# The expert weights of a two-block layer, laid out in memory in the order in which the kernel loads them

## The chip, the cores and the metric

The kernel runs on one core of one Trainium2 chip. The metric is device time in microseconds (us) of one execution; lower is better. All data are fp32. A "chunk" below is one transfer of 1 MB (1,048,576 bytes) of weights from memory into a tile of 128 partitions with 8 KB each.

## The reference, cut to what matters

Two transformer blocks are applied to 256 tokens of width 1024. The second block ends in a mixture of 32 experts; each token goes to two of them. What the change touches is only this part:

```python
N_EXPERTS, EXPERT_TOPK, EXPERT_FF, D_MODEL = 32, 2, 512, 1024

def hier_moe(h, w_group, b_group, w_expert, b_expert, w1, w3, w2):
    # w1, w3: (32, 1024, 512); w2: (32, 512, 1024)
    ...
    def expert_block(args):
        xb, e = args
        hid = jax.nn.silu(xb @ w1[e]) * (xb @ w3[e])
        return hid @ w2[e]
    ...
```

The three expert tensors hold 3 x 32 x 1024 x 512 numbers, 192 chunks of 1 MB. Every execution reads all of them once.

## The kernel before

The program first computes block one, then the attention part of block two, then the router, and then walks over the experts in 8 groups of 4 (`for g in range(8)`, L1102). Tokens sit in 32 slots for each expert, so 4 experts fill the 128 columns of TensorE: `slot_mm` (L1090) issues 4 matmuls, one for each expert of the group, each on its own 32 columns, all with the same k-slice of the weights.

One group needs 24 chunks, in this order: 8 of w1 and 8 of w3 (one for each slice of 128 input features, each with 4 experts x 512 columns), then 4 of w2 for the first 512 output columns and 4 for the last 512. The last group (g = 7) takes its last 512 columns in two passes of 256 (`FINE`, L1098), so that its last 4 MB come as 8 transfers of 512 KB.

All expert weights come through `eload` (L1031). It takes the next tile of a rotation over 19 tiles of 8 KB per partition (`rings`, L825) and issues one transfer from the SP queue (L1034). The first group also finds two extra places for its last two w3 chunks; one of them is filled by two half transfers (`whalf`). SP issues in program order and waits, before a transfer, until the last reader of the tile is through. The order of instructions is chosen by a scheduler at build time. Some expert transfers are issued early, between loads of other weights (`wload`, L148); the others follow after SP has loaded the number `cnt` (L1047), which decides at g = 4 whether the branch for overfull experts (`overflow`, L1046) is taken. It was not taken in this execution.

The transfer itself is this:

```python
t = t[:, :ne * n].rearrange("p (e n) -> p e n", e=ne)
nc.sync.dma_start(out=t, in_=wd[g * 4 + e0:g * 4 + e0 + ne, k * P:(k + 1) * P,
                                c0:c0 + n].rearrange("e p n -> p e n"))
```

With n = 512 each partition receives four rows of 2 KB, one from each expert; in memory these rows lie 2 MB apart. With n = 256 (the last 8 transfers) the rows have 1 KB.

After the last expert chunk, PE finishes the last 256 columns, the last norm follows (L1163 to L1173), and two transfers write the result (L1174).

Of the kernel before, what the change touches and what calls it, by code (L numbers as in the profile page):

```python
# [18 lines left out]
P = 128  # L19
# [62 lines left out]
def block_kernel(ctx: ExitStack, tc: tile.TileContext, A, out: bass.AP):  # L82
# [22 lines left out]
    def t_tile(n):  # L105
        return psum.tile([P, 512], F32, name=n, tag="t", bufs=2)
# [28 lines left out]

    # weight chunks rotate over the slots that are open
    slots_of = {"list": [(ring, 4)], "i": 0}
# [19 lines left out]

    # operand pieces: rotate over the pools that are open
    base = (None, 3)
# [3 lines left out]
    def piece(v, a, b, after=(), eng=None):  # L163
        order = [p for p, n in homes["list"] for _ in range(n)]
        bufs = dict(homes["list"])
        pair = order[homes["i"] % len(order)]
        homes["i"] += 1
        if pair is None:
            # two pieces in a row share a slot for their low parts
            hi = dn.tile([P, a, b], F32R, name="whi", tag="whi", bufs=3)  # L170
            if low["n"] % 2 == 0:
                low["t"] = lows.tile([P, 2, 1024], F32R, name="wlo", tag="w")
            lo = low["t"][:, low["n"] % 2, :a * b].rearrange("p (a b) -> p a b", a=a)
            low["n"] += 1
        else:
            hi = pair.tile([P, a, b], F32R, name="whi", tag="whi", bufs=bufs[pair])
            lo = pair.tile([P, a, b], F32R, name="wlo", tag="wlo", bufs=bufs[pair])
        with ExitStack() as q:
            for ins in after:
                q.enter_context(tc.issue_after(ins.ins))  # L180
            split_to(hi, lo, v, eng)
        return hi, lo
# [8 lines left out]

    # features out on partitions: weights stationary, all tokens stream
    def t_block(dst, pc, c0, k, act):
# [10 lines left out]

    # tokens out on partitions: tokens stationary, weights stream
    def ts_pieces(src, c0, n, after=(), free=0, aside=()):
# [116 lines left out]

    # ------------------------------------------------------------------ first block: mixing
    w_in = A["w_in"][0]
# [25 lines left out]

    # pool mixer
    po = (mg1.tile([P, 4, S], F32R, name="poh"), mg1.tile([P, 4, S], F32R, name="pol"))
# [33 lines left out]

    # memory keys and values
    w = wload(rows(w_in, 0, KT, 2048, 256), KT, 256)
# [14 lines left out]

    # stick-breaking attention, keys on partitions
    sb = (mg1.tile([P, 4, S], F32R, name="sbh", tag="sbh"), mg1.tile([P, 4, S], F32R, name="sbl", tag="sbl"))
# [33 lines left out]

    # cross attention
    xo = (mg1.tile([P, 2, S], F32R, name="xoh"), mg1.tile([P, 2, S], F32R, name="xol"))
# [36 lines left out]

    # gated branches  # L480
    tg = {}
# [56 lines left out]

    # ------------------------------------------------------------------ feed-forward
    s1 = ExitStack()  # L540
# [20 lines left out]

    # first columns token-major, so that the first half of the tokens can run ahead
    h0 = (fp.tile([P, 4, S], F32R, name="h0h", bufs=1), fp.tile([P, 4, S], F32R, name="h0l", bufs=1))
# [46 lines left out]

    # ------------------------------------------------------------------ second block: mixing
    s2 = ExitStack()
# [47 lines left out]

    # index scores
    qiT = rope_heads(3072, 1.0, "qiT", at, 4, first[0], 2, (1,3))
# [126 lines left out]

    # router weights, with the gain of the norm before them  # L790
    wr = perm.tile([P, KT, 40], F32, name="wr")
# [41 lines left out]

    # ------------------------------------------------------------------ second block: experts
    nt = xp.tile([P, NT, D], F32, name="nt", tag="xhi")
# [161 lines left out]

    # gates
    nneg = ptile([P, NT, 2], "nneg")
# [27 lines left out]

    w1d, w3d, w2d = A["w1_2"][0], A["w3_2"][0], A["w2_2"][0]
    slots_of.update(list=rings, i=0)

    def eload(wd, g, k, c0, n):  # L1031
        def fill(t, e0, ne):
            t = t[:, :ne * n].rearrange("p (e n) -> p e n", e=ne)
            nc.sync.dma_start(out=t, in_=wd[g * 4 + e0:g * 4 + e0 + ne, k * P:(k + 1) * P,  # L1034
                                            c0:c0 + n].rearrange("e p n -> p e n"))
            return [t[:, e, :] for e in range(ne)]

        # places that only the first group's weights find free
        if g == 0 and wd is w3d and k == KT - 1:
            return fill(xp.tile([P, 2048], F32, name="wchunk", tag="xlo"), 0, 4)  # L1040
        if g == 0 and wd is w3d and k == KT - 2:
            return [r for e0 in (0, 2) for r in fill(dn.tile([P, 1024], F32, name="whalf", tag="whi", bufs=3), e0, 2)]
        return fill(chunk_tile(), 0, 4)

    # experts with more than CAP tokens: the tokens past the slots, over all experts
    def overflow():  # L1046
        cv = nc.values_load(cnt[0:1, 0:1], min_val=0, max_val=S)  # L1047
        with tc.If(cv > CAP):
# [11 lines left out]
            ow = dn.tile([P, D], F32, name="ovw", tag="whi", bufs=3)  # L1060
            with tc.For_i(0, NE, 1) as ei:
                for f in range(4):
                    bs = []
                    for wd in (w1d, w3d):
                        wt = ow.rearrange("p (k n) -> p k n", k=KT)
                        nc.gpsimd.dma_start(out=wt, in_=wd[bass.ds(ei, 1), :, f * P:(f + 1) * P].rearrange(
                            "o (k p) n -> p (o k) n", p=P))
                        b = t_tile("ovb")
                        for kt in range(KT):
                            nc.tensor.matmul(b[:, :S], lhsT=wt[:, kt, :], rhs=xT[:, kt, :], start=(kt == 0),  # L1070
                                             stop=(kt == KT - 1))
                        bs.append(b)
                    s = dn.tile([P, 512], F32, name="ms", tag="sqscr", bufs=1)
                    nc.scalar.activation(s[:, :S], bs[0][:, :S], AF.Silu)
                    nc.vector.tensor_tensor(out=hh[:, f, :], in0=bs[1][:, :S], in1=s[:, :S], op=ALU.mult)
                for hf in range(2):
                    o = acc_tile("ovo")
                    for f in range(4):
                        wt = ow[:, (f % 2) * 512:(f % 2 + 1) * 512]
                        nc.gpsimd.dma_start(out=wt, in_=w2d[bass.ds(ei, 1), f * P:(f + 1) * P,  # L1080
                                                          hf * 512:(hf + 1) * 512].rearrange("o p n -> p (o n)"))
                        for tt in range(NT):
                            nc.tensor.matmul(o[tt], lhsT=hh[:, f, tt * P:(tt + 1) * P], rhs=wt, start=(f == 0),
                                             stop=(f == 3))
                    for tt in range(NT):
                        xa = x[:, tt, hf * 512:(hf + 1) * 512]
                        nc.vector.scalar_tensor_tensor(out=xa, in0=o[tt], scalar=gov[:, tt, bass.ds(ei, 1)],
                                                       in1=xa, op0=ALU.mult, op1=ALU.add)

    def slot_mm(o, lhsT, w, first, last):  # L1090
        for e in range(4):
            ps = slice(e * 32, e * 32 + 32)
            nc.tensor.matmul(o[ps, :], lhsT=lhsT[:, ps], rhs=w[e], start=first, stop=last,  # L1093
                             skip_group_check=True, tile_position=(0, e * 32))

    # the last columns come in small parts, so that little is left to do behind the last weights
    WHOLE = ((0, 512), (512, 512))
# [4 lines left out]
    for g in range(8):  # L1102
# [4 lines left out]
        hb = acc_tile("hb")  # L1107
        for i, wd in enumerate((w1d, w3d)):
            for kt in range(KT):
                slot_mm(hb[i], xs[:, kt, :], eload(wd, g, kt, 0, EFF), kt == 0, kt == KT - 1)  # L1110
        s = dn.tile([P, 512], F32, name="ms", tag="sqscr", bufs=1)
# [22 lines left out]
        if g == 7:  # L1134
            # the gain of the last norm, on all partitions
            glx = xp.tile([P, 2, D], F32, name="glx", tag="xhi")
# [9 lines left out]
        for i, (c0, n) in enumerate(FINE if g == 7 else WHOLE):  # L1146
            cs = slice(c0, c0 + n)
            yb = t_tile("yb")
            for ft in range(4):
                slot_mm(yb[:, :n], hT[:, ft, :], eload(w2d, g, ft, c0, n), ft == 0, ft == 3)  # L1150
            nc.scalar.activation(y[:, cs], yb[:, :n], AF.Copy)  # L1151
# [11 lines left out]
    for tt in range(NT):  # L1163
# [15 lines left out]
        "w_in_2", "w_proj_a_2", "w_proj_b_2", "w_out_2", "g_ffn_2", "w_group_2", "b_group_2", "w_expert_2",  # L1179
        "b_expert_2", "w1_2", "w3_2", "w2_2", "g_final_2"]  # L1180
_OUTS = [((1, 256, 1024), "float32")]


# [17 lines left out]
```

## Time and profile before

| what | value |
|---|---|
| median of 3 runs | 1135.88 us (1135.5 to 1139.17) |
| span of the profiled execution | 1139.4 us |
| PE busy | 969.1 us (85%) |
| DVE busy | 447.6 us (39%) |
| ACT busy | 354.5 us (31%) |
| read from memory | 308.70 MB, 272 GB/s over the span |
| time of the packets on the SP transfers' queue | 77.0% of 16 DMA engines |

The profiled execution's span lies at the upper end of the three timed runs, 3.5 us above their median. PE's busy time is the sum of intervals in which some matmul was in its pipeline; it says little about a stage in which matmuls wait for each other's data. The page's second part cuts the span into 40 slices of 28.5 us and shows for each the busy share of the engines, the granted TensorE clock (PEclk, tenths of 2.4 GHz), the busy share of the 16 DMA engines and the rate of their transfers. The experts fill the last 17 of these slices.

### The profile page before, as it was taken

The numbers are of one execution on the slowest core, as the hardware profiler recorded it, in microseconds if no ns is written. First come the engines' busy times: TensorE is split into PE (matmuls) and PEld (weight loads), VectorE is DVE, ScalarE is ACT, GpSimd is POOL, SyncE is SP. The second block draws the span as 40 slices with busy tenths as digits, with TensorE's granted clock in tenths as the row PEclk, the third lists the DMA queues.
The fourth block names the chain that finished last, engine by engine and source line by source line (L and its number), as shares of the span: only waits on it lengthen the run. The fifth ranks groups of instructions, "written<-read, shape, count | busy, mean of one in ns | idle before, by whom it ended". The sixth has DMA issues, their size and how long they took to land. (4 is left out here: it accounts for less than half of the span.)

```text
span 1139.4 us, 14755 instructions
## 1 busy us (share of the span) xinstructions
PE 969.1 (85%) x6119; PEld 662.9 (58%) x6119; DVE 447.6 (39%) x750; ACT 354.5 (31%) x552; POOL 53.3 (5%) x45
## 2 busy tenths in 40 slices
PE   6999999999999998999999996875676676676665
PEld 5889989978999986788889842121121222112111
DVE  5555536676455446698547511100101010001102
ACT  4445655365444434445654410000000000000002
POOL 1000012120000003120000000000000000000000
PEclk9999999999999999999999999766778778767767
DMA  9844337767555326545457999999999999999996
GB/s 318 264 150 148 112 130 248 241 232 243 191 190 187 121 90 222 170 162 186 150 192 268 370 319 386 386 387 385 387 386 384 386 385 387 385 387 386 387 387 215
DMA packets 181349, 310.74 MB, mean 273 GB/s; under 512 B 11040, under 2 KB 62240, under 8 KB 181280
## 3 DMA queue, kind: packets, MB, share of 16 engines
q1 hardware_dynamic: 181280, 309.77, 77.0%
q8 instruction: 49, 0.80, 0.3%
q14 instruction: 20, 0.16, 0.0%
HBM read 308.70 MB, written 1.05 MB: 272 GB/s over the span
## 5 line engine op out<-in xcount | busy, mean ns | idle before, releaser
L156 DVE TENSOR_TENSOR wlo<-wchunk,whi 128x1024 fp32r<-128x1024 f32 (+1 forms) x180 | 222.9, 1240 | 160.0 <-ACT whi L155 157.5
L155 ACT ACTIVATE whi<-wchunk 128x1024 fp32r<-128x1024 f32 (+1 forms) x193 | 200.7, 1048 | 226.6 <-PE gu L186 55.8
L1093 PE MATMUL hb<-wchunk,xs 128*32 128x512 f32 x1016 | 168.5, 765 | 95.2 <-DMA wchunk<-in_w_dram 91.6
L1093 PEld LDWEIGHTS hb<-wchunk,xs 128*32 128x32 f32 x1016 | 26.3, 121 | 216.5 <-DMA wchunk<-in_w_dram 175.9
L1093 PE MATMUL yb<-wchunk,mw 128*32 128x512 f32 (+1 forms) x544 | 75.5, 672 | 31.3 <-DMA wchunk<-in_w_dram 29.1
L185 PE MATMUL gate<-xhi,whi 128*128 128x256 f32 x320 | 92.0, 287 | 0.6 <-DVE tg L508 0.6
L186 PE MATMUL gate<-xlo,whi 128*128 128x256 f32 x320 | 91.4, 286 | 0.0
L187 PE MATMUL gate<-xhi,wlo 128*128 128x256 f32 x320 | 91.3, 285 | 0.0
L187 PE MATMUL gu<-xhi,wlo 128*128 128x256 f32 x288 | 81.3, 282 | 0.0
L186 PE MATMUL gu<-xlo,whi 128*128 128x256 f32 x288 | 81.2, 282 | 0.0
L185 PE MATMUL gu<-xhi,whi 128*128 128x256 f32 x288 | 81.1, 282 | 0.0
L1156 DVE TENSOR_TENSOR x<-x,comb 128x512 f32<-128x512 f32 (+1 forms) x34 | 22.3, 656 | 140.5 <-PE comb L1154 140.5
L1093 PEld LDWEIGHTS yb<-wchunk,mw 128*32 128x32 f32 x544 | 14.8, 122 | 86.5 <-DMA wchunk<-in_w_dram 57.3
L185 PEld LDWEIGHTS gate<-xhi,whi 128*128 128x128 f32 x320 | 61.1, 191 | 3.4 <-issue 2.4
L1120 ACT ACTIVATE mw<-hT 128x512 f32<-128x512 f32 x8 | 4.8, 597 | 184.6 <-PE hT L1118 184.6
L987 DVE TENSOR_TENSOR xs<-gat,gk 128x512 f32<-128x512 f32 x16 | 11.1, 692 | 130.0 <-PE gat L979 130.0
L186 PEld LDWEIGHTS gate<-xlo,whi 128*128 128x128 f32 x320 | 61.1, 191 | 1.4 <-issue 1.3
L187 PEld LDWEIGHTS gate<-xhi,wlo 128*128 128x128 f32 x320 | 61.0, 191 | 1.4 <-issue 1.4
L185 PEld LDWEIGHTS gu<-xhi,whi 128*128 128x128 f32 x288 | 55.1, 191 | 0.3
L186 PEld LDWEIGHTS gu<-xlo,whi 128*128 128x128 f32 x288 | 54.8, 190 | 0.3
L187 PEld LDWEIGHTS gu<-xhi,wlo 128*128 128x128 f32 x288 | 54.8, 190 | 0.0
L1115 DVE TENSOR_TENSOR mw<-hb,ms 128x512 f32<-128x512 f32 x8 | 5.5, 692 | 115.8 <-PE hb L1093 115.8
(395 smaller groups left out, 1710.5 us busy)
## 6 DMA issues: line engine op xcount, KB each, us to landing
wchunk<-in_w_dram SPq DMA_DIRECT2D x187, 1024.0 KB, 14.4
wchunk<-in_w_in_dram SPq DMA_DIRECT2D x43, 1024.0 KB, 5.1
wchunk<-in_w_ffn_in_dram SPq DMA_DIRECT2D x22, 1024.0 KB, 5.2
wchunk<-in_w_ffn_out_dram SPq DMA_DIRECT2D x11, 1024.0 KB, 5.0
wchunk<-in_w_out_dram SPq DMA_DIRECT2D x8, 1024.0 KB, 5.9
wchunk<-in_w_dram SPq DMA_DIRECT2D x8, 512.0 KB, 9.2
wchunk<-in_w_mem_kv_dram SPq DMA_DIRECT2D x2, 1024.0 KB, 5.5
wchunk<-in_w_pool_o_dram SPq DMA_DIRECT2D x2, 1024.0 KB, 5.3
```

What stands on the lines that cost most here:

```text
L155: a = nc.scalar.activation(hi, src, AF.Copy)
L156: return a, (eng or nc.vector).tensor_tensor(out=lo, in0=src, in1=hi.bitcast(F32), op=ALU.subtract)
L185: nc.tensor.matmul(o, lhsT=lh[0], rhs=rh[0], start=start, stop=False)
L186: nc.tensor.matmul(o, lhsT=lh[0], rhs=rh[1], start=False, stop=False)
L187: return nc.tensor.matmul(o, lhsT=lh[1], rhs=rh[0], start=False, stop=stop)
L987: nc.vector.tensor_tensor(out=xss[g][:, ks, :], in0=b.rearrange("p (k t) -> p k t", k=4), in1=gk[:, ks, None].to_broadcast([P, 4, P]), op= ...
L1093: nc.tensor.matmul(o[ps, :], lhsT=lhsT[:, ps], rhs=w[e], start=first, stop=last, skip_group_check=True, tile_position=(0, e * 32))
L1115: nc.vector.tensor_tensor(out=h, in0=hb[1], in1=s, op=ALU.mult)
L1120: nc.scalar.activation(mw[:, 1, :], b, AF.Copy)
L1156: nc.vector.tensor_tensor(out=xa, in0=xa, in1=cb[:, :n], op=ALU.add)
```

## The change

A new function `expert_runs` rearranges the three expert tensors on the host, before the kernel starts, into one tensor `experts` of 192 pieces, each 128 x 2048 numbers, in the order (group, chunk). The device time does not contain it. For 20 of the 24 chunks of a group each partition's 8 KB lie in one run. For the 4 chunks of the last 512 output columns the piece is split into two halves of 256 columns, and each partition receives two runs of 4 KB; the last group loads these halves one at a time, as 512 KB with one run of 4 KB for each partition. Bytes, number of transfers, destination tiles and their rotation stay as they were. The two half transfers of the first group (`whalf`) now read runs of 4 KB.

In `slot_mm` the weights of an expert are now a view with one more dimension: (128, 1, 512), or (128, 2, 256) with the two pieces 4 KB apart in the tile. The `overflow` branch, not taken here, is rewritten to read the new tensor; its loop has 8 rounds with the work of 4 experts each instead of 32 rounds.

```diff
-    w1d, w3d, w2d = A["w1_2"][0], A["w3_2"][0], A["w2_2"][0]
+    ew = A["experts"].rearrange("(g c) p n -> g c p n", g=8)
+    W1, W3, W2 = 0, KT, 2 * KT
...
-    def eload(wd, g, k, c0, n):
+    def eload(g, c, part=None):
+        src = ew[g, c]
+        if c >= W2 + 4:
+
+            src = src.rearrange("p n -> (p n)").rearrange("(h p n) -> p h n", h=2, p=P)
+            if part is not None:
+                src = src[:, part:part + 1, :]
+
         def fill(t, e0, ne):
-            t = t[:, :ne * n].rearrange("p (e n) -> p e n", e=ne)
-            nc.sync.dma_start(out=t, in_=wd[g * 4 + e0:g * 4 + e0 + ne, k * P:(k + 1) * P,
-                                            c0:c0 + n].rearrange("e p n -> p e n"))
-            return [t[:, e, :] for e in range(ne)]
...
+            if c >= W2 + 4:
+                m = 2 if part is None else 1
+                v = t[:, :m * 1024].rearrange("p (h n) -> p h n", h=m)
+                nc.sync.dma_start(out=v, in_=src)
+                v = v.rearrange("p h (e n) -> p h e n", e=4)
+                return [v[:, :, e, :] for e in range(4)]
+            v = t[:, :ne * 512]
+            nc.sync.dma_start(out=v, in_=src[:, e0 * 512:(e0 + ne) * 512])
+            return [v[:, e * 512:(e + 1) * 512].rearrange("p (h n) -> p h n", h=1) for e in range(ne)]
...
     def slot_mm(o, lhsT, w, first, last):
         for e in range(4):
             ps = slice(e * 32, e * 32 + 32)
-            nc.tensor.matmul(o[ps, :], lhsT=lhsT[:, ps], rhs=w[e], start=first, stop=last,
-                             skip_group_check=True, tile_position=(0, e * 32))
...
+            m = w[e].shape[1]
+            nc.tensor.matmul(o[ps, :].rearrange("p (h n) -> p h n", h=m), lhsT=lhsT[:, ps], rhs=w[e], start=first,
+                             stop=last, skip_group_check=True, tile_position=(0, e * 32))
...
-                slot_mm(hb[i], xs[:, kt, :], eload(wd, g, kt, 0, EFF), kt == 0, kt == KT - 1)
+                slot_mm(hb[i], xs[:, kt, :], eload(g, c0 + kt), kt == 0, kt == KT - 1)
...
+def expert_runs(w1, w3, w2):
+
+    a = [w.reshape(8, 4, KT, P, EFF).transpose(0, 2, 3, 1, 4).reshape(8, KT, P, 2048) for w in (w1, w3)]
+    v = w2.reshape(8, 4, 4, P, 2, 512).transpose(0, 4, 2, 3, 1, 5)
+    lo = v[:, 0].reshape(8, 4, P, 2048)
+    hi = v[:, 1].reshape(8, 4, P, 4, 2, 256).transpose(0, 1, 4, 2, 3, 5).reshape(8, 4, P, 2048)
+    return np.concatenate([*a, lo, hi], axis=1).reshape(8 * 24, P, 2048)
```

No engine's instructions change place: the transfers stand where they stood between the other loads. This piece of SP's order, from the attention part of block two, shows it (rows with - are those of before, with + those after; a row names line, destination, source and the shape of one transfer).

```order
 L148 DMA wchunk<-in_w_in_dram 128x4x512 x2
-L1034 DMA wchunk<-in_w_2_dram 128x4x512 x2
+L1049 DMA wchunk<-in_experts_dram 128x2048 x2
 L148 DMA wchunk<-in_w_in_dram 128x4x512 x9
 L148 DMA wchunk<-in_w_in_dram 128x8x256 x4
-L1034 DMA wchunk<-in_w_2_dram 128x4x512
+L1049 DMA wchunk<-in_experts_dram 128x2048
 L148 DMA wchunk<-in_w_in_dram 128x8x256 x4
```

The shape is what moved: 128 partitions with four pieces of 512 numbers became 128 partitions with one piece of 2048. In both orders SP issues, after it has loaded `cnt`, 94 whole chunks ahead of the branch at g = 4, 72 behind it, and then the 8 transfers of 512 KB; 22 MB have been issued ahead of `cnt`.

## Rows read from the trace of the kernel before

**Rows 1.** The page's slices: granted clock and DMA share in tenths, rate, 28.5 us each.
```profile
PEclk9999999999999999999999999766778778767767
DMA  9844337767555326545457999999999999999996
GB/s 318 264 150 148 112 130 248 241 232 243 191 190 187 121 90 222 170 162 186 150 192 268 370 319 386 386 387 385 387 386 384 386 385 387 385 387 386 387 387 215
```

**Rows 2.** Waits from 655 us on: total us, times, longest us.
```profile
PEld hb L1093 <- DMA wchunk<-in_w_dram: 175.9, 71, 11.5
...
PE hb L1093 <- DMA wchunk<-in_w_dram: 91.6, 65, 10.6
PEld yb L1093 <- DMA wchunk<-in_w_dram: 57.3, 36, 2.9
```

**Rows 3.** Windows of the expert part: length, busy times, granted clock, DMA share, GB/s.
```profile
core 0: us, PE busy (x) PEld busy (x) DVE busy (x) ACT busy (x) POOL busy (x), PEclk, DMA share, GB/s
...
660.00:662.00 2.00, 2.00 (x24) 0.56 (x20) 0.00 (x0) 0.00 (x0) 0.00 (x0) 1.00 0.97 298
662.00:664.00 2.00, 2.00 (x24) 0.65 (x20) 0.00 (x0) 0.00 (x0) 0.00 (x0) 1.00 1.08 238
664.00:666.00 2.00, 2.00 (x24) 0.60 (x20) 0.00 (x0) 1.49 (x2) 0.00 (x0) 1.00 0.86 292
666.00:668.00 2.00, 2.00 (x24) 0.57 (x20) 0.00 (x0) 0.39 (x1) 0.00 (x0) 1.00 1.05 363
700.00:1100.00 400.00, 269.41 (x1430) 74.62 (x1428) 37.80 (x70) 14.33 (x24) 0.00 (x0) 0.74 1.05 386
...
1122.00:1124.00 2.00, 0.86 (x14) 0.16 (x8) 1.11 (x2) 1.00 (x3) 0.00 (x0) 1.00 1.08 365
```

**Rows 4.** DMA packets and bytes, 700 to 1100 us; issues with us to landing.
```profile
DMA packets 77639, 154.41 MB, mean 386 GB/s; under 512 B 2351, under 2 KB 2351, under 8 KB 77622
...
q1 hardware_dynamic: 77622, 154.16, 104.6%
...
wchunk<-in_w_dram SPq DMA_DIRECT2D x147, 1024.0 KB, 14.4
```

**Rows 5.** SP's wait for `cnt` and the transfers behind it, timeline.
```profile
658.44 42.17 SPq L1034 DMA_DIRECT2D wchunk<-in_w_dram  x18
```

**Rows 6.** Other weights: DMA slices, packets and issues, 366 to 385 us.
```profile
GB/s 0 0 69 69 190 414 414 448 423 181 0 0 17 0 78 95 103 414 414 414 423 267 0 0 0 0 129 78 354 414 431 414 371 52 0 0 0 29 152 233
DMA packets 961, 3.37 MB, mean 177 GB/s; under 512 B 63, under 2 KB 191, under 8 KB 959
...
wchunk<-in_w_ffn_out_dram SPq DMA_DIRECT2D x3, 1024.0 KB, 4.9
```

**Rows 7.** Windows ahead of the experts: two expert chunks, then w_ffn_out and w_out.
```profile
240.00:243.50 3.50, 3.50 (x17) 2.85 (x16) 3.50 (x3) 3.50 (x4) 2.91 (x2) 1.00 1.05 399
246.00:250.00 4.00, 3.91 (x17) 2.85 (x17) 3.33 (x6) 1.44 (x2) 0.56 (x1) 1.00 1.03 422
605.00:607.00 2.00, 2.00 (x19) 2.00 (x18) 1.32 (x2) 0.39 (x1) 0.00 (x0) 1.00 1.02 418
608.00:610.00 2.00, 2.00 (x19) 2.00 (x18) 2.00 (x4) 1.09 (x2) 0.00 (x0) 1.00 1.02 414
```

**Rows 8.** Expert matmuls in the timeline, first at 2.4 GHz, then at 1.2 GHz.
```profile
678.21 7.05 PE L1093 MATMUL yb<-wchunk,mw 128*32 128x512 f32 x64
...
714.93 1.93 PE L1093 MATMUL hb<-wchunk,xs 128*32 128x512 f32 x8 [0.79 <-DMA wchunk<-in_w_dram]
```

**Rows 9.** The chain that ended last, one group's pieces: start, us, what.
```profile
889.94 1.93 PE hb L1093 x8
891.87 2.75 PE gat L979 x13
...
910.87 0.70 DVE mw L1115
911.62 1.13 PE hT L1118 x4
912.77 0.61 ACT mw L1120
```

**Rows 10.** Groups of instructions from 655 us on: count, busy us, mean ns.
```profile
L1154 PE MATMUL comb<-ysb,mw 128*128 128x512 f32 x60 | 38.6, 773 | 8.1 <-ACT ysb L1151 8.1
```

**Rows 11.** The chain's end, from the last expert transfer on.
```profile
1120.20 8.43 DMA wchunk<-in_w_dram
1128.67 0.68 PE yb L1093 x8
...
1134.16 0.93 ACT fo L1173
```

**Rows 12.** Who held up the SP queue from 655 us on: us, times, longest us.
```profile
SPq L1034 <- PE hb L1093: 131.1, 75, 4.6
...
SPq L1034 <- PE comb L1154: 32.5, 14, 4.7
...
SPq L1047 <- DVE cnt L1026: 4.5, 1, 4.5
```

More of the change, by code (lines that the diff above doesn't have):

```diff
@@ L1026, in block_kernel @@
     nc.vector.tensor_copy(cnt, cmx)
-    w1d, w3d, w2d = A["w1_2"][0], A["w3_2"][0], A["w2_2"][0]
+    ew = A["experts"].rearrange("(g c) p n -> g c p n", g=8)
+    W1, W3, W2 = 0, KT, 2 * KT
     slots_of.update(list=rings, i=0)
-    def eload(wd, g, k, c0, n):
-        def fill(t, e0, ne):
-            t = t[:, :ne * n].rearrange("p (e n) -> p e n", e=ne)
-            nc.sync.dma_start(out=t, in_=wd[g * 4 + e0:g * 4 + e0 + ne, k * P:(k + 1) * P,
-                                            c0:c0 + n].rearrange("e p n -> p e n"))
-            return [t[:, e, :] for e in range(ne)]
-        if g == 0 and wd is w3d and k == KT - 1:
+    def eload(g, c, part=None):
[4 more added lines that the diff above has]
+                src = src[:, part:part + 1, :]
+        def fill(t, e0, ne):
+            if c >= W2 + 4:
[7 more added lines that the diff above has]
+            return [v[:, e * 512:(e + 1) * 512].rearrange("p (h n) -> p h n", h=1) for e in range(ne)]
+        if g == 0 and c == W3 + KT - 1:
             return fill(xp.tile([P, 2048], F32, name="wchunk", tag="xlo"), 0, 4)
-        if g == 0 and wd is w3d and k == KT - 2:
+        if g == 0 and c == W3 + KT - 2:
             return [r for e0 in (0, 2) for r in fill(dn.tile([P, 1024], F32, name="whalf", tag="whi", bufs=3), e0, 2)]
@@ L1060, in overflow @@
             ow = dn.tile([P, D], F32, name="ovw", tag="whi", bufs=3)
[L1061 to L1077, printed above, removed]
-                    for f in range(4):
-                        wt = ow[:, (f % 2) * 512:(f % 2 + 1) * 512]
-                        nc.gpsimd.dma_start(out=wt, in_=w2d[bass.ds(ei, 1), f * P:(f + 1) * P,
-                                                          hf * 512:(hf + 1) * 512].rearrange("o p n -> p (o n)"))
-                        for tt in range(NT):
[L1083 to L1088, printed above, removed]
@@ new lines, in overflow @@
+            gv = gov.rearrange("p t (g e) -> p t g e", g=8)
+            with tc.For_i(0, 8, 1) as gi:
+                for e in range(4):
+                    for f in range(4):
+                        bs = []
+                        for c0 in (W1, W3):
+                            wt = ow.rearrange("p (k n) -> p k n", k=KT)
+                            cs = slice(e * 512 + f * P, e * 512 + (f + 1) * P)
+                            nc.gpsimd.dma_start(out=wt, in_=ew[bass.ds(gi, 1), c0:c0 + KT, :, cs].rearrange(
+                                "o k p n -> p (o k) n"))
+                            b = t_tile("ovb")
+                            for kt in range(KT):
+                                nc.tensor.matmul(b[:, :S], lhsT=wt[:, kt, :], rhs=xT[:, kt, :], start=(kt == 0),
+                                                 stop=(kt == KT - 1))
+                            bs.append(b)
+                        s = dn.tile([P, 512], F32, name="ms", tag="sqscr", bufs=1)
+                        nc.scalar.activation(s[:, :S], bs[0][:, :S], AF.Silu)
+                        nc.vector.tensor_tensor(out=hh[:, f, :], in0=bs[1][:, :S], in1=s[:, :S], op=ALU.mult)
+                    for hf in range(2):
+                        o = acc_tile("ovo")
+                        for f in range(4):
+                            wt = ow[:, (f % 2) * 512:(f % 2 + 1) * 512]
+                            src = ew[bass.ds(gi, 1), W2 + hf * 4 + f]
+                            if hf == 0:
+                                src = src[:, :, e * 512:(e + 1) * 512].rearrange("o p n -> p (o n)")
+                                nc.gpsimd.dma_start(out=wt, in_=src)
+                            else:
+                                src = src.rearrange("o p n -> o (p n)").rearrange("o (h p n) -> p (o h) n", h=2, p=P)
+                                nc.gpsimd.dma_start(out=wt.rearrange("p (h n) -> p h n", h=2),
+                                                    in_=src[:, :, e * 256:(e + 1) * 256])
+                            for tt in range(NT):
+                                nc.tensor.matmul(o[tt], lhsT=hh[:, f, tt * P:(tt + 1) * P], rhs=wt, start=(f == 0),
+                                                 stop=(f == 3))
+                        for tt in range(NT):
+                            xa = x[:, tt, hf * 512:(hf + 1) * 512]
+                            nc.vector.scalar_tensor_tensor(out=xa, in0=o[tt], scalar=gv[:, tt, bass.ds(gi, 1), e],
+                                                           in1=xa, op0=ALU.mult, op1=ALU.add)
@@ L1107, in block_kernel @@
         hb = acc_tile("hb")
-        for i, wd in enumerate((w1d, w3d)):
+        for i, c0 in enumerate((W1, W3)):
             for kt in range(KT):
-                slot_mm(hb[i], xs[:, kt, :], eload(wd, g, kt, 0, EFF), kt == 0, kt == KT - 1)
+                slot_mm(hb[i], xs[:, kt, :], eload(g, c0 + kt), kt == 0, kt == KT - 1)
         s = dn.tile([P, 512], F32, name="ms", tag="sqscr", bufs=1)
@@ L1149, in block_kernel @@
             for ft in range(4):
-                slot_mm(yb[:, :n], hT[:, ft, :], eload(w2d, g, ft, c0, n), ft == 0, ft == 3)
+                w = eload(g, W2 + (4 if c0 else 0) + ft, c0 // 256 - 2 if n == 256 else None)
+                slot_mm(yb[:, :n], hT[:, ft, :], w, ft == 0, ft == 3)
             nc.scalar.activation(y[:, cs], yb[:, :n], AF.Copy)
@@ L1179 @@
         "w_in_2", "w_proj_a_2", "w_proj_b_2", "w_out_2", "g_ffn_2", "w_group_2", "b_group_2", "w_expert_2",
-        "b_expert_2", "w1_2", "w3_2", "w2_2", "g_final_2"]
+        "b_expert_2", "g_final_2"]
 _OUTS = [((1, 256, 1024), "float32")]
+def expert_runs(w1, w3, w2):
[4 more added lines that the diff above has]
+    return np.concatenate([*a, lo, hi], axis=1).reshape(8 * 24, P, 2048)
 def kernel(**inputs):
@@ L1190 @@
     named = [(n, np.ascontiguousarray(inputs[n])) for n in _INS]
+    named.append(("experts", expert_runs(*(np.asarray(inputs[n]) for n in ("w1_2", "w3_2", "w2_2")))))
     named += [(f"c{i}", a) for i, a in enumerate(_CONSTS)]
```

## The prediction

> **What bounds the kernel now.** I began with the page's slices [rows 1]. The last 17 of the 40 slices are the experts: there the transfer rate stands at 384 to 387 GB/s, slice after slice, with the DMA engines' share at 9 and over, while the granted clock of TensorE lies at 6 to 8 tenths. Nowhere earlier does the rate hold such a level. A flat rate under a changing clock says that the stage runs at the pace of the transfers. The waits from 655 us on say the same from the other side [rows 2]: PE's matmuls and weight loads of the experts wait for landing chunks, 71 times for w1 and w3 alone, up to 11.5 us at a time. The windows [rows 3] give the size: 386 GB/s over the 400 us from 700 to 1100, DMA share 1.05 (over 1 because an engine's packets overlap a little), clock 0.74. In this window 154.41 MB arrived [rows 4]; 77,622 - 2,351 = 75,271 packets of 2 KB and over make 154.15 MB, so they are the 2 KB rows. One chunk of 1.0486 MB takes 400 x 1.0486 / 154.41 = **2.716 us**, a group of 24 takes 65.2 us.
>
> The stage does not begin with the first expert chunk. 22 MB come early, beside a PE that is still busy with attention and the router; then SP waits for `cnt`, and only from 658.44 us on do the other 170 MB follow [rows 5]. What makes transfers faster before that moment is given back in the wait for `cnt`, which hangs on the router, not on DMA. So the change is worth what it does to 166 whole chunks and 8 halves.
>
> **What the row length is worth.** The trace has no 8 KB row in this queue. It has 4 KB rows: w_ffn_out and w_out come as two rows of 4 KB for each partition. Between 366 and 385 us three such chunks come alone (961 packets in all, 768 of them of 4 KB), and their slices of 0.475 us read 414, 414, 448, 423 and again 414, 414, 414, 423 [rows 6]. Longer windows in such transfers read 422, 418 and 414 [rows 7]. Two expert chunks of 2 KB rows, loaded just ahead of the first of these, read 399 in 3.5 us [rows 7], and over hundreds of us 386 [rows 3]: a short stretch shows some 3% more than a long one. The 1 KB rows of the end read 365 [rows 3]. So the rate rises with the row, 365, 386 to 399, 414 to 422: each row seems to cost something beside its bytes.
>
> Per engine (a sixteenth of the rate), a 2 KB row takes 2048 x 16 / 386 = 84.9 ns in the long run. A 4 KB row at 418 takes 156.8 ns; lowered by the 3% of long stretches (405 GB/s) it takes 161.8. The second 2 KB thus cost 71.9 to 76.9 ns instead of 84.9. If the third and fourth cost as much, 8 KB take 300.6 to 315.6 ns, which is 436 to 415 GB/s. Bounds: at least what long stretches of 4 KB rows should give (405: no further gain), at most 436. I take **420 GB/s** for 8 KB, near the value from long stretches because the whole stage is one, and **410** for 4 KB.
>
> A rule stands against the change. The Trainium skill, page "DMA: Bandwidth & Descriptors", section "Specifications", calls 512 bytes the least transfer for line rate; by it 2 KB rows are there already and the sum is 0. The trace disagrees: 2 KB rows hold 386 where 4 KB rows reach 414 to 422 [rows 3, 7]. The same page, section "Why small descriptors are slow", charges a fixed 3 cycles per packet on 32-byte beats; with its ceiling of 435 GB/s (an estimate) 2 KB would reach 416 and 8 KB 430, a gain of 3.3%, some 15 us here. The measured step from 2 KB to 4 KB alone is larger.
>
> **The sum.** A group has 20 chunks at 420 (2.497 us) and 4 at 410 (2.558 us), 2.507 us in the mean, 0.209 less than 2.716.
> - 166 whole chunks x 0.209 = 34.7 us.
> - From 660 to 668 us the rate is below 386 (298, 238, 292, 363) [rows 3]: first the tiles of the early chunks have to come free. These 2.3 chunks may gain nothing: minus 0.5 us.
> - 8 halves (4.19 MB) go from 1 KB rows to 4 KB rows: 4.19 MB at 365 is 11.5 us, at 410 10.2 us: 1.3 us.
> - The end behind the last landing (1120.20 + 8.43 = 1128.6 us to the end of the span [rows 11]) holds the same instructions: 0.
> - The matmuls of the last 512 columns read two pieces 4 KB apart, the others one. I take 0, since PE waits for each chunk anyway; cover and price follow below.
> - The rewritten branch is not taken; its longer code is only jumped over, at g = 4, under transfers in flight of 14.4 us [rows 4]: 0.
>
> Together **35.5 us**. The profiled span of 1139.4 us becomes 1103.9. The span is 3.5 us above the median of the runs; set against the median, 1135.9 - 35.5 = **1100.4 us**.
>
> **Does PE keep up?** At 2.4 GHz eight chunks (64 matmuls) take 7.05 us, 0.88 each; at 1.2 GHz one chunk takes 1.93 us [rows 8]. A whole group at 1.2 GHz: 24 x 1.93 = 46.3; 32 `gat` matmuls at 2.75 / 13 us each = 6.8; the transposes `hT` and as much again for the gates, 2.2; `comb` 38.6 us over 7.5 groups' worth (60 records, 8 for a group) = 5.1, more at the low clock only; the chain through DVE and ACT 1.3 [rows 9, 10]. That is 62 us against 60.2 us of transfers. At 2.4 GHz it is about half. The mean of 0.74 lies between, so PE has room, and when it falls behind it no longer waits, which is the state in which it had the high clock (7.05 us for 64 matmuls without a gap).
>
> SP waits for tiles, 131.1 us for PE's w1 and w3 matmuls alone, but never over 4.7 us at a time [rows 12], while 14.4 us of transfers are in flight [rows 4]. At 2.507 us for a chunk the same 5.3 chunks cover 13.3 us, so the queue should not run dry.
>
> **Rivals.**
> 1. *8 KB rows run no faster than 4 KB rows*, because a row is cut into pieces on its way or the gain levels off. For it: no row over 4 KB stands in this queue. At 405 a chunk takes 2.589 us, the gain is 166 x 0.127 = 21 us plus 1: about 1114 us; at 410, 1109 us.
> 2. *No gain: memory or the tile's side sets 386, not the row.* Then the time stays at 1136 us. For it: 386 is remarkably flat. Against it: 414 to 422 in the same tiles from the same memory. By the 512-byte rule cited above it would come to this.
> 3. *PE becomes the bound* at a low clock: 62 us for a group instead of 65.2, over 7 groups 22 us less, about 1114 us; with wide gaps between chunks on top, 1120 us. Against it: the clock of 1.00 whenever PE works through landed chunks (the windows from 660 to 668 us) [rows 3].
> 4. *Slower: the 16 engines, each reading its own 64 KB of one contiguous MB in step, collide in memory*; in the 2 KB layout their rows lay in four experts. From 662 to 664 us there is a rate of 238 at a DMA share of 1.08 [rows 3], so engines can be busy and slow. It decides once the rate falls below 386; at 370 a chunk takes 2.834 us, 166 x 0.118 = 20 us more, about 1155 us. Against it: w_ffn_out and w_out, whose 512 KB pieces are contiguous too, reach 414 to 422.
>
> **How the numbers follow.** Forecast (8 KB rows at 410 to 434, which gives 1087 to 1108 us): 0.70. Rival 1 (1108 to 1116 us): 0.13. Rival 2: 0.07. Rival 3: 0.06. Rival 4: 0.04. The predicted time is the forecast's, 1100.4 us. The range 1087 to 1116 us holds the forecast, rival 1 and part of rival 3. Faster by more than 0.3% (about what a measurement of this kernel can tell from no change): 0.70 + 0.13 + 0.06 = 0.89; within: 0.07; slower: 0.04.
>
> **What the profile after would show.** Right: the slices of the experts at 415 to 425 GB/s; some 128 packets a chunk instead of 512; a group of 24 chunks in about 60 us; the start of the stream still near 658 us; the same 10 us or so behind the last landing; the granted clock a little higher than 0.74. Packets of 4 KB at about 410 would mean rival 1, a rate still at 386 rival 2, a DMA share clearly below 1 between 700 and 1050 us rival 3, and a rate under 386 with a share over 1 rival 4. The prediction goes wrong above all if the cost of a row beside its bytes is not the same for 8 KB as between 2 and 4 KB, for which the trace has no row.

## The result and the profile after

The changed kernel takes **1097.27 us** (median of 4 runs, 1095.6 to 1099.06) against 1135.91 us for the kernel before: a ratio of 0.9649, with a 95% interval of 0.9631 to 0.9667, 38.6 us less. Forecast were 1100.4 us, with a range of 1087 to 1116. The profiled execution has a span of 1093.9 us; before it was 1139.4.

The page's slices after, the counterpart of [rows 1], 27.3 us each:

```profile
PEclk9999999999999999999999999887888877887879
DMA  9844347567555533645546789999999999999996
GB/s 330 276 157 155 116 135 251 194 238 262 191 192 190 165 101 112 228 153 181 166 171 238 305 302 420 419 419 422 416 421 417 418 416 421 418 419 420 417 422 269
```

The expert slices stand at 416 to 422 GB/s where they stood at 384 to 387. The stage is still flat, so it is still the transfers that pace it; the granted clock is a little higher, at 7 to 8 tenths in most slices. PE still waits for landing chunks about as often as in [rows 2], only for less time in all (us in total, times, longest us):

```profile
PEld hb L1117 <- DMA wchunk<-in_experts_dram: 156.4, 70, 9.2
```

Ahead of the experts the slices look much as before.

The windows after, the counterpart of [rows 3] (columns as there):

```profile
660.00:662.00 2.00, 2.00 (x24) 0.59 (x20) 0.00 (x0) 1.52 (x2) 0.00 (x0) 1.00 1.06 444
662.00:664.00 2.00, 2.00 (x24) 0.57 (x20) 0.00 (x0) 0.00 (x0) 0.00 (x0) 1.00 1.00 406
664.00:666.00 2.00, 2.00 (x24) 0.52 (x16) 0.00 (x0) 0.00 (x0) 0.00 (x0) 1.00 1.04 434
...
700.00:1050.00 350.00, 244.14 (x1376) 66.88 (x1376) 36.35 (x68) 14.33 (x24) 0.00 (x0) 0.80 1.02 419
```

And the packets and issues of 700 to 1050 us, the counterpart of [rows 4]:

```profile
DMA packets 22811, 146.64 MB, mean 419 GB/s; under 512 B 2236, under 2 KB 2236, under 8 KB 7612
...
wchunk<-in_experts_dram SPq DMA_DIRECT2D x140, 1024.0 KB, 19.9
```

The rows of weights are 22,811 - 2,236 = 20,575 packets for 140 chunks, 147 a chunk: 20 chunks with 128 and 4 with 256 give 149. Of them 22,811 - 7,612 = 15,199 hold 8 KB. So a row of 8 KB travels as one packet, and no row is cut up. A chunk takes 350 x 1.0486 / 146.64 = 2.503 us instead of 2.716, a group 60.1 us instead of 65.2. What is new is the time from issue to landing, 19.9 us instead of 14.4: eight chunks are under way at once instead of five.

Nearly all of this stands in the expert part, but not all of the 45.5 us between the two profiled spans belongs to the change. The first row below is of the kernel before, the second of the changed kernel: the updates of x at the ends of block one's halves, with the first and last start at the end of the times.

```profile
L315 DVE SCALAR_TENSOR_TENSOR x<-pn,rsr,x x8: 739/748/2907, 231.5 to 435.6; 128x512 f32<-128x512 f32 x8
```
```profile
L315 DVE SCALAR_TENSOR_TENSOR x<-pn,rsr,x x8: 737/750/2904, 227.9 to 431.9; 128x512 f32<-128x512 f32 x8
```

The changed kernel is 3.6 us ahead at 231.5 us already, before it has issued its first expert transfer (at 233.1 us by its own clock, 236.8 before). No transfer of the change has run by then; the experiments below come back to it. It is a reason for the profiled spans to differ by more than the medians of the runs.

### The profile page after: what moved, and what is told of

It is laid out like the page before. It is cut to its first block, busy times and chain, and to the rows that moved or that the text cites. A ratio compares the mean times of both kernels' runs of the same rounds, so it can differ in the third digit from the quotient of the medians.

```text
span 1093.9 us, 14757 instructions
## 1 busy us (share of the span) xinstructions
PE 946.4 (87%) x6119; PEld 653.5 (60%) x6119; DVE 447.5 (41%) x750; ACT 354.4 (32%) x552; POOL 52.9 (5%) x45
## 4 chain that ended last, share of the span: by engine, by line
PE 57%; DMA 37%; DVE 3%; ACT 1%; issue 1%; SPq 1%; POOL 0%; POOLq 0%; ACTq 0%; DVEq 0%
DMA wchunk<-in_experts_dram 36%; PE gate L185 4%; PE gu L186 4%; PE gu L185 4%; PE gu L187 4%; PE gate L187 4%; PE gate L186 4%; PE hb L1117 2%; PE fo L185 2%; PE fo L187 2%; PE fo L186 2%; PE y L185 1%; PE y L187 1%; PE y L186 1%; PE wo L185 1%; PE wo L186 1%
## 5 line engine op out<-in xcount | busy, mean ns | idle before, releaser
L1117 PE MATMUL hb<-wchunk,xs 128*32 128x512 f32 x1016 | 162.6, 739 | 80.5 <-DMA wchunk<-in_experts_dram 75.1
L1117 PE MATMUL yb<-wchunk,mw 128*32 128x512 f32 (+1 forms) x544 | 71.6, 639 | 24.5 <-DMA wchunk<-in_experts_dram 21.8
## 6 DMA issues: line engine op xcount, KB each, us to landing
wchunk<-in_experts_dram SPq DMA_DIRECT2D x187, 1024.0 KB, 19.9
wchunk<-in_experts_dram SPq DMA_DIRECT2D x8, 512.0 KB, 14.4
```

The lines of the kernel that those rows point to most:

```text
L1117: nc.tensor.matmul(o[ps, :].rearrange("p (h n) -> p h n", h=m), lhsT=lhsT[:, ps], rhs=w[e], start=first, stop=last, skip_group_check=True, ...
```

## The experiments

**The row alone.** Three kernels keep the chunks of the changed kernel, each one contiguous MB, and change only the length of its rows: a chunk is stored as R blocks of 128 rows, so that each partition gets R rows of 8/R KB.

```diff
-    ew = A["experts"].rearrange("(g c) p n -> g c p n", g=8)
+    ew = A["experts"].rearrange("(g c) r p n -> g c r p n", g=8)
...
+            nc.sync.dma_start(out=v.rearrange("p (r n) -> p r n", r=k),
+                              in_=ew[g, c, r0:r0 + k].rearrange("r p n -> p r n"))
```

Rows of 2 KB (R = 4):

> Each chunk is one contiguous MB of memory as in the changed kernel, but stored as four blocks of 128 rows, so that each partition again gets four rows of 2 KB, now 256 KB apart instead of 2 MB. Theory (the length of a row sets its cost; where the rows lie does not): about 386 GB/s over 700 to 1100 us, as before the change, and 1134 to 1137 us. Rival (what counts is that a chunk lies together in memory): about 419 GB/s and 1097 us. A time between them would share the gain out between the two.

Measured: 1133.09 us, ratio 0.9969 (0.9956 to 0.9981). This row is its window of 700 to 1050 us:

```profile
700.00:1050.00 350.00, 238.57 (x1272) 67.23 (x1272) 33.91 (x63) 13.13 (x22) 0.00 (x0) 0.73 1.05 386
```

The rate is that of the kernel before to the digit shown, although every chunk now lies together. Lying together is not what the change gained from. Two small places give this kernel about half of its 4 us over the one before: its last 8 transfers have rows of 2 KB instead of 1 KB (10.7 us from the landing of the last whole chunk to that of the last half, where the kernel before needs 11.6), and the stream starts without the slow first transfers (below; about 1 us). Where the rest comes from was not traced.

Rows of 4 KB (R = 2):

> As the changed kernel, but every chunk is stored as two blocks of 128 rows, so that all chunks come as two rows of 4 KB for each partition. Theory with a fixed cost per row: 2 KB rows at 386 GB/s and the changed kernel's 2.503 us for a chunk (20 of 24 with 8 KB rows, 4 with 4 KB) give about 9.4 ns per row and engine beside 37.7 ns per KB; 4 KB rows then take 160.3 ns, 2.565 us for a chunk, 409 GB/s, and 166 x 0.062 = 10 us more than the changed kernel: 1107 us, between 1105 and 1110. Rival (only lying together counts): 1097 us. Rival (SP's making of descriptors is the bound, in proportion to the number of rows): no longer a bound from 4 KB on, so again 1097 us.

Measured: 1108.26 us, ratio 0.9750 (0.9729 to 0.9771), and 409 GB/s:

```profile
700.00:1050.00 350.00, 242.97 (x1344) 66.24 (x1348) 35.73 (x67) 13.73 (x23) 0.00 (x0) 0.77 1.03 409
```

Rows of 1 KB (R = 8):

> As the changed kernel, but each chunk is stored as eight blocks of 128 rows of 1 KB. Theory with a fixed cost per row (9.4 ns beside 37.7 ns per KB): 47.1 ns for a row, 3.017 us for a chunk, 347 GB/s, about 1184 us. If the number of rows alone set the time (a bound in making descriptors, 2.5 us for 512 rows), a chunk would take 5 us and the run over 1500 us. If only lying together counts: 1097 us.

Measured: 1186.14 us (one run), and 348 GB/s:

```profile
700.00:1050.00 350.00, 221.16 (x1140) 58.40 (x1138) 30.08 (x58) 11.34 (x19) 0.00 (x0) 0.71 1.10 348
```

Both came out within some 2 us of the law. A bound in proportion to the number of rows alone is out: from 256 rows in a chunk to 1024 it would have cost four times as much, and the chunk went from 2.56 to 3.01 us.

**Rows of 8 KB, far apart.** Here the memory order is group, partition, chunk:

```diff
+    ew = A["experts"].rearrange("(g p) c n -> g c p n", g=8)
...
+    return images(w1, w3, w2).transpose(0, 2, 1, 3).reshape(8 * P, 24, 2048)
```

> Rows of 8 KB as in the changed kernel, for the last 512 columns too (except the 8 halves of the end, 4 KB), but the rows of one chunk lie 192 KB apart: the memory order is group, partition, chunk. Theory (row length alone): 28 chunks of 4 KB rows become 8 KB rows at 2.490 instead of 2.565 us, so 2 us less than the changed kernel, 1095 us, and 421 GB/s. Rival (lying together counts): well above 1097 us, up to 1136. Two pieces 4 KB apart in the operand of the last 512 columns are kept, so they are not what differs.

Measured: 1095.23 us, ratio 0.9630 (0.9611 to 0.9649), and 421 GB/s:

```profile
700.00:1050.00 350.00, 240.99 (x1379) 65.39 (x1376) 35.85 (x68) 14.33 (x24) 0.00 (x0) 0.80 1.01 421
```

Row length alone gives the whole gain, at a pitch of 192 KB as well as in one block. That also answers the rival in which 16 engines reading one contiguous MB in step would collide: they run at the same rate in both layouts.

**What would be next.** This kernel loads half of each chunk and lets two experts of a group share the weights of the other two. Its last 512 columns come in one piece, as in the version at the end of this section:

```diff
+            m = ne // 2
+            v = t[:, :m * 512]
+            nc.sync.dma_start(out=v, in_=ew[g, c, :, e0 * 512:(e0 + m) * 512])
+            return [v[:, e % m * 512:(e % m + 1) * 512].rearrange("p (h n) -> p h n", h=1) for e in range(ne)]
```

> As the changed kernel, but only half of each expert chunk is loaded (512 KB, one row of 4 KB for each partition), and the matmuls of experts 3 and 4 of a group use the weights of experts 1 and 2; so half of the expert weights is left out of the computation. It shows what would bound the stage if transfers cost half. Transfers by the cost per row: 16 engines, 8 rows of 160 ns, 1.28 us for a chunk, 31 us for a group. Theory (PE regains 2.4 GHz when it doesn't wait): PE needs 24 x 0.88 = 21 us for the expert matmuls and some 11 for the rest, so 31 to 35 us for a group and 900 to 945 us in all, with a granted clock near 1.0. Rival (PE stays at 1.2 GHz for long): up to 62 us for a group, and 1100 us or more, hardly below the changed kernel.

Measured: 919.63 us (one run). A window of the expert part and three successive rows of DVE's product of the two projections, one for each group:

```profile
700.00:880.00 180.00, 171.29 (x1308) 66.34 (x1308) 35.19 (x65) 13.73 (x23) 0.00 (x0) 0.99 0.99 385
```
```profile
669.37 0.69 DVE L1124 TENSOR_TENSOR mw<-hb,ms 128x512 f32<-128x512 f32 x1 [13.27 <-PE hb L1102]
700.28 0.69 DVE L1124 TENSOR_TENSOR mw<-hb,ms 128x512 f32<-128x512 f32 x1 [6.29 <-PE hb L1102]
731.21 0.69 DVE L1124 TENSOR_TENSOR mw<-hb,ms 128x512 f32<-128x512 f32 x1 [6.29 <-PE hb L1102]
```

A group takes 30.9 us in this stretch, PE is busy for 171.29 of 180 us, and its granted clock is 0.99 where it is 0.80 in the changed kernel, in which PE waits for chunks. PE does the work of a group in half the time that the transfers of the changed kernel need. So PE was no bound in the changed kernel. With half the bytes both are near their limits. The rates of the same 180 us in 40 slices of 4.5 us, and the time from issue to landing in us (last number), are

```profile
GB/s 413 410 404 410 409 412 408 409 403 411 406 411 410 411 404 382 333 415 84 177 294 412 417 405 409 409 412 410 408 403 410 356 387 408 413 411 368 371 400 396
...
wchunk<-in_experts_dram SPq DMA_DIRECT2D x129, 512.0 KB, 8.4
```

In the first 15 slices the transfers still run at the 409 GB/s or so of 4 KB rows, at which 24 half chunks take 30.8 us, as long as PE is busy with a group. The two rows answer one more rival. In the changed kernel 8.3 MB are under way (419 GB/s for 19.9 us) where 5.6 MB were (386 for 14.4), so the rate might have risen because more is under way and not because the rows are longer. Here 3.4 MB are under way (409 for 8.4 us), less than in the kernel before, and the rate is the 409 of the kernel with 4 KB rows, which has 7.6 MB under way (18.6 us).

**What the early transfers are worth.** The kernel before, with the first group alone in the new order:

```diff
+            if g == 0:
+                c = k + (0 if wd is w1d else KT if wd is w3d else 2 * KT + c0 // 128)
+                nc.sync.dma_start(out=t, in_=A["group0"][c, :, e0 * 512:(e0 + ne) * 512].rearrange(
+                    "p (e n) -> p e n", e=ne))
+                return [t[:, e, :] for e in range(ne)]
```

> The kernel before, with only the 24 chunks of the first group in the new order (8 KB rows); 22 of these are issued ahead of the wait for cnt. Theory (what arrives early is given back in the wait for cnt): no change beyond 0.3% from this part; at most 1 to 3 us less if the slow first transfers behind the wait belong to the old layout of the first group. Rival (early transfers with longer rows free the way for the attention's weights): the router starts earlier and the run is some 5 us shorter.

Measured: 1134.21 us, ratio 0.9978 (0.9968 to 0.9987), 1.5 to 3.6 us less. Beside it the kernel before was profiled once more:

> The kernel before, profiled once more. It shows how much two executions of one kernel differ ahead of the experts: in the first profile of before, block one was 3.6 us later than in the profile of the changed kernel even before the first expert transfer. Expected if that was the execution and not the change: the first update of x by the post-norm anywhere between 227.9 and 231.5 us, 1135 to 1139 us in all. It also shows whether the slow first transfers behind the wait for cnt (238 to 363 GB/s in the windows of 2 us from 660 to 668) belong to this layout: then they come again, some 2.5 us of lost transfers; else they were this one execution.

Measured: 1139.47 us (one run). Its first update of x starts at 231.4 us, close to the first profile's 231.5. But the changed kernel, profiled a second time (below), has it at 229.9 instead of 227.9, and rows of 1 KB, which are new in layout too, at 231.0. So the time of block one moves by 2 us and more between executions, with no order by row length; whether the place of the other tensors in memory has a part in it was not tried. From there to the router's scaling of x (`nt`, L927) every kernel needs 413.8 to 415.0 us, and the kernel before has both ends of this itself (415.0 and 413.9), so the early transfers gain nothing that shows, as forecast. What the new order of the first group gains, 2.5 us, must lie behind the router.

The second profile of before does show its slow start again, in the windows behind the wait for `cnt` (which ends at 657.16 us here):

```profile
658.00:660.00 2.00, 2.00 (x24) 0.59 (x20) 0.00 (x0) 0.00 (x0) 0.00 (x0) 1.00 0.88 246
660.00:662.00 2.00, 2.00 (x24) 0.57 (x20) 0.00 (x0) 0.00 (x0) 0.00 (x0) 1.00 1.02 272
662.00:664.00 2.00, 2.00 (x24) 0.65 (x20) 0.00 (x0) 0.78 (x1) 0.00 (x0) 1.00 0.88 294
664.00:666.00 2.00, 2.00 (x24) 0.59 (x20) 0.00 (x0) 1.10 (x2) 0.00 (x0) 1.00 0.98 321
```

PE is equally busy there in every kernel; what differs is the layout of the transfers. The first two behind the wait are the last chunks of group one's w2. One more kernel stores only the 4 chunks of these columns together, with rows of 2 KB as ever:

```diff
+            if g == 0 and wd is w2d and c0:
+                nc.sync.dma_start(out=t, in_=A["group0_hi"][k].rearrange("e p n -> p e n"))
+                return [t[:, e, :] for e in range(ne)]
```

> The kernel before, in which only the 4 chunks of the first group's last 512 columns are stored together, as four blocks of 128 rows of 2 KB, 256 KB apart (in the kernel before: rows with a pitch of 4 KB, from four experts 2 MB apart). Two of them are the first transfers behind the wait for cnt, which ran at 238 to 363 GB/s in both profiles of the kernel before, and no slower than 350 once the first group lay in 8 KB rows or all chunks lay together in 2 KB rows. Theory (those two chunks are slow because of how their rows lie): the windows of 2 us there rise to about 390, and the run is about 2.5 us shorter than before, ratio 0.9978. Rival (any transfer in the old layout starts slowly after a pause): the next chunks, in the old layout, take the slow start over, and the ratio is 1.

Measured: 1136.12 us, ratio 0.9991 (0.9982 to 1.0000). The profile shows what was expected:

```profile
658.00:660.00 2.00, 2.00 (x24) 0.61 (x20) 0.00 (x0) 0.00 (x0) 0.00 (x0) 1.00 0.93 357
660.00:662.00 2.00, 2.00 (x24) 0.56 (x20) 0.00 (x0) 0.08 (x1) 0.00 (x0) 1.00 1.05 403
662.00:664.00 2.00, 2.00 (x24) 0.65 (x20) 0.00 (x0) 1.80 (x2) 0.00 (x0) 1.00 1.05 389
664.00:666.00 2.00, 2.00 (x24) 0.60 (x20) 0.00 (x0) 0.00 (x0) 0.00 (x0) 1.00 1.06 389
```

The next chunks, in the old layout, run at full rate. So the slow start is tied to how these two chunks lie. But the runs show 0 to 2 us where 2.5 were expected. Counted from SP's first issue behind the wait, 9.56 us of the kernel before, of this kernel and of the changed kernel read:

```profile
658.44:668.00 9.56, 9.56 (x92) 2.86 (x88) 0.00 (x0) 1.88 (x2) 0.00 (x0) 1.00 0.87 259
```
```profile
655.86:665.42 9.56, 9.56 (x92) 2.86 (x88) 0.00 (x0) 1.88 (x2) 0.00 (x0) 1.00 0.83 306
```
```profile
653.58:663.14 9.56, 9.56 (x92) 2.86 (x88) 0.00 (x0) 1.88 (x2) 0.00 (x0) 1.00 0.89 342
```

From 259 to 306 GB/s are 0.45 MB, 1.2 us at 386. The 2.5 us counted as lost what a stream needs to get going in any layout: the changed kernel too has only 342 there of its later 419. Why the two chunks are slow in this place, and chunks of the same shape are not slow later, at 386 GB/s, was not tried.

**A version that is a little better.** The last 512 columns as rows of 8 KB too; only the last group keeps its halves, in a small tensor of their own.

```diff
+            if part is not None:
+                v = t[:, :1024]
+                nc.sync.dma_start(out=v, in_=A["halves"][c - W2 - 4, part])
+                return [v[:, e * 256:(e + 1) * 256].rearrange("p (h n) -> p h n", h=1) for e in range(4)]
```

> As the changed kernel, but the last 512 columns too come as rows of 8 KB in groups 1 to 7 (the two halves are kept apart only for the last group, in a small tensor of their own), and the matmuls read one piece of 512 numbers again. Theory (9.4 ns for each row saved): 28 chunks at 2.490 instead of 2.565 us, 2.1 us less than the changed kernel: 1095 us, 421 GB/s, as with the rows of 8 KB lying far apart. If the two pieces in the operand had a price of their own, more than that.

Measured: 1094.92 us, ratio 0.9632 (0.9618 to 0.9646), 421 GB/s. Then again, on one chip with the changed kernel:

> The changed kernel itself, beside the version with 8 KB rows for the last 512 columns on the same chip. Expected: 0.965 of before, as in its first measurement.

> 8 KB rows for the last 512 columns too, on the same chip as the changed kernel. Theory (9.4 ns for each row saved, 28 chunks): 2.1 us less than the changed kernel, 0.2%; it should show as a difference between the two medians, near the limit of what 5 rounds can tell.

Measured there: 1098.32 us, ratio 0.9663 (0.9649 to 0.9677), for the changed kernel and 1095.91 us, ratio 0.9643 (0.9629 to 0.9656), for the version with 8 KB rows throughout: 2.4 us less where 2.1 were expected. The intervals overlap, so the ratios alone don't settle it; but four of the five runs of this version (1094.6 to 1097.3 us) lie below all five of the changed kernel (1097.75 to 1099.26), and the profiles have it at 421 against 419 GB/s each time. Rows 8 KB long but far apart gave the same 1095 us with the operand in two pieces, so the two pieces have no price of their own that these runs can see.

## Why the prediction was right

**The bound and the law behind the sum.** The stage was paced by transfers, and the term "166 whole chunks x 0.209" measured 166 x (2.716 - 2.503) = 35.4 us against 34.7. The two rates that were chosen, 420 GB/s for 8 KB rows and 410 for 4 KB, measured 421 and 409. That they were met within 1 GB/s is partly luck: the working gave 415 to 436 for 8 KB, and 405 for 4 KB, and the choice of 410 has no working of its own. Worked out per engine, a sixteenth of the rate, from the windows above:

| row | GB/s | time of a row | of this beside the bytes |
|---|---|---|---|
| 1 KB | 348 | 47.1 ns | 9.3 ns |
| 2 KB | 386 | 84.9 ns | 9.3 ns |
| 4 KB | 409 | 160.2 ns | 9.0 ns |
| 8 KB | 421 | 311.3 ns | 8.9 ns |

The last column takes 37.8 ns for each KB off, the slope that fits the four times. Each row costs about 9 ns whatever its length, at these four lengths; what the 9 ns are spent on, no run shows. The bytes themselves would pass at 434 GB/s (16 x 1024 / 37.8). The Trainium skill, page "DMA: Bandwidth & Descriptors", section "Where 436 GB/s comes from", puts the ceiling at 435 GB/s, and the 434 worked out here agree. The rule of the Trainium skill, same page, section "Specifications", that 512 bytes suffice for line rate, which the prediction set against the change, does not hold here: 1 KB rows reach 80% of that ceiling, 2 KB rows 89%. The choice of a rate "near the value from long stretches" was the one that mattered: short windows, taken at their word, would have given 436.

**The terms around it.** The 8 halves gave what was forecast: from the landing of the last whole chunk to that of the last half, 11.6 us became 10.1, where 11.5 and 10.2 were expected. The wrong step is "These 2.3 chunks may gain nothing: minus 0.5 us". The slow windows from 660 to 668 us had been put down to tiles that were not yet free. They were slow transfers: SP began its fifth issue behind the wait at 661.9 us, and the first of the five landed only at 665.6, 7.1 us after its issue where the changed kernel needs 4.9. In the 9.56 us shown above the kernel before moves 2.48 MB, 6.4 us of work at its later 386 GB/s, and the changed kernel 3.27 MB, 7.8 us at 419: 1.4 us gained instead of 0.5 us withheld. Behind the last landing the term 0 was 0.6 us off, 10.1 us instead of 10.7: the last four `comb` matmuls took 1.13 us at a granted clock of 1.00 (2.4 GHz), before 2.07 us at 0.50 (1.2 GHz). The prediction had not reckoned with that.

The sum, then: from the router's scaling of x to the end the profiled executions need 452.2 us (1093.9 - 641.7) against 492.9 (1139.4 - 646.5), 40.7 us less. Of this 35.4 are the chunks, 1.4 the start, 1.4 the halves and 0.6 the end. About 2 us are left. They lie inside the stream: from the third landing behind the wait to that of the last whole chunk the kernel before needs 445.6 us and the changed kernel 408.9, 36.7 less, where 163 chunks at 0.213 us give 34.7. What holds the landings up there was not traced. The second pair of profiles has 39.8 (492.1 and 452.3). The runs' medians differ by 38.6. Against the 40.7 of the profiles the forecast of 35.5 was 5 us short: 1.9 at the start, 0.7 in the chunks, 0.6 at the end and these 2 us; against the medians it was 3 us short.

**The cover.** "The queue should not run dry" was right, in another way than argued. Before, SP waited for tiles [rows 12]; now it waits for its own transfers:

```profile
SPq L1049 <- DMA wchunk<-in_experts_dram: 239.6, 123, 3.4
SPq L1045 <- DMA wchunk<-in_experts_dram: 66.0, 32, 2.2
```

With eight chunks under way the next transfer is issued when the first of them has landed. That holds nothing up, since eight chunks are 20 us of transfers.

**The rivals.** Rows cut on their way: out, by the packets. No gain: out, by the rate. PE as the bound: out, by the kernel with half the bytes. More bytes under way: out, by the same kernel. Collision of engines in one contiguous MB: out, by the far rows.

## What to carry to other kernels

Where a stage runs at a flat transfer rate, divide the time by the rows, not only by the bytes: here each row cost 9 ns of its engine beside 37.8 ns for each KB, so 2 KB rows left 11% of the ceiling unused and 8 KB rows 3%. Over the long stretch only the length of the row counted, not whether the rows of a transfer lie together (2 KB rows in one MB or 2 MB apart, 8 KB rows in one MB or 192 KB apart; other places were not tried). So here it was enough to store the weights so that what one partition receives in one transfer is one run. Two lengths that other loads of the same kernel happen to use were enough to bound the rate of a third one (415 to 436, measured 421). What kept the forecast near the lower bound, where the measured rate lies, was to set a short window of 2 KB rows against long ones first, and to lower the short windows of 4 KB rows by the difference.

## What the hardware showed beside this

In a full queue, the time that SP spends on issuing one chunk follows the rows. First the kernel before's 195 whole and half transfers, then the whole chunks with 8 KB rows of the changed kernel (least, median and longest time in ns):

```profile
L1034 SPq DMA_DIRECT2D wchunk<-in_w_dram x195: 367/2534/4825, 236.8 to 1120.2; - x195
```
```profile
L1049 SPq DMA_DIRECT2D wchunk<-in_experts_dram x159: 327/328/4312, 233.1 to 1053.8; - x159
```

With 2 KB rows SP stays in the issue for 2.5 us, almost the time of the chunk itself, and 14.4 us of transfers are under way; with 8 KB rows it is through after 0.33 us and 19.9 us are under way. With 4 KB rows the issue still takes 2.3 us in the median, and the cost per row is the same 9 ns on both sides of this step from 2.3 to 0.33 us. That speaks against the long issue as what sets the rate; SP then only stands behind a full queue, though no run tried what fills it.
